# Moving the operands of the matmuls to other byte offsets in a Trainium2 layer kernel

## The chip, the cores and the metric

One core of one Trainium2 chip runs the whole kernel. The metric is the device time of one execution in microseconds, the median of several runs; less is better. TensorE does the matmuls (each is a weight load of the stationary operand and a pass of the moving one), VectorE and ScalarE work on tiles in SBUF, and SyncE issues the DMAs.

## The reference

One layer of an encoder in float32, for one sequence of 512 tokens and a width of 2048:

```python
mod = silu(c) @ w_ada + b_ada                       # six rows of 2048: sh1, sc1, g1, sh2, sc2, g2
h = rms_norm(x, norm1_g) * (1.0 + sc1) + sh1
proj = h @ w_in                                     # 2048 x 7168
o = concatenate([hgrn2(proj[:, :4096]), stick_breaking(proj[:, 4096:])])   # 8 heads each
x = x + g1 * (o @ w_out)                            # 2048 x 2048
h = rms_norm(x, norm2_g) * (1.0 + sc2) + sh2
gate, up = split(h @ w_ffn_in)                      # 2048 x 2*5632
x = x + g2 * ((silu(gate) * up) @ w_ffn_out)        # 5632 x 2048
```

## The kernel before

Every large product is computed from split operands: a float32 tile is copied by ScalarE into a rounded `hi` part and VectorE subtracts to get the `lo` part (`split`, lines 212 to 222, for weights; `split_o` and `split_to` for activations). Each product is then three matmuls of type float32r: hi by hi, hi by lo, lo by hi (`three`, line 227; `product`, line 908; `multiply`, line 1183). Every matmul has its own weight load.

The stages, in order of time: the values of the recurrent heads (banks `st`), the projections of the eight attention heads (`sb_project`, tiles `sbp`) with the attention work of the head before put between the matmuls, the projections of the eight recurrent heads (`hg_project`, `hg_gate`, tiles `hgf`, `hgq`, `hgg`) with the recurrent work between them, the output projection (`wo_part`), the first two column tiles of the feed-forward input (`first_part`, weights `wff`), the other 42 (`for f in range(2, FM)`, with a seven-product scheme after Strassen: products 1 to 7 of 24 matmuls with 256 columns), and the feed-forward output (`multiply`, again seven products, 12 units of 3 or 4 blocks). The order is written out by hand, with a clock of estimated times (`Clock`, `Timed`) that decides where the attention steps go.

Which operand is stationary differs. In `st` and `sbp` the activations `hhi`/`hlo` are stationary and the weights move (512 and 384 columns); in `hgf`, `hgq`, `hgg`, `wo` the weights are stationary and the activations (`hhi`/`hlo`, then `ohi`/`olo`) move, 512 columns; in the feed-forward input the weights are stationary and the operand blocks `opA` to `opD` move, 256 columns; in the feed-forward output the forms `opsA` to `opsC` are stationary and the weights move, 512 columns.

All these tiles lie in pools with fixed places in a partition. Pools on the left are stacked upwards: `const`, the weights' pool `wp` (four `raw` slots of 8192 bytes, three `hi` and three `lo` slots of 4096), then `hp` (slots `hhi` and `hlo`, 32,768 bytes each, used in turn by the split activations, the split output rows, `opB`/`opC` and `opsC`/`opsB`), then `fh` (slot `b1`: `opA`, later `opsA`) and `fg` (slot `b22`: `opD`). Pools on the right end at byte 229,344 and are stacked downwards. Each tile's size is rounded up to 32 bytes. The `hi` slots start at 43,808, 47,904 and 52,000, the `lo` slots at 56,096, 60,192 and 64,288, `hhi` at 68,384, `hlo` at 101,152, `b1` at 133,920, `b22` at 166,688: all 32 past a multiple of 256. Every block inside a tile is a multiple of 512 bytes long, so this holds for the start of every operand in them.

In the loop over `f` every fourth split of weights goes to a spare pair, `hi2` and `lo2` (`spare_here`, lines 1105 and 1106), in the right-hand pool `tp` at 215,008 and 219,104: 224 past a multiple of 256. The names in the trace show which: `ff_1h` and `ff_1l` are the ordinary tiles of product 1, `ff_1hi` and `ff_1lo` the spare pair. In the output stage the spare pair is a part of `opsB` that is not needed yet (`more`, line 1163, and `spare_there`, line 1165).

Of the kernel before, what the change touches and what calls it, by code (L numbers as in the profile page):

```python
# [10 lines left out]
F32 = mybir.dt.float32  # L11
F32R = mybir.dt.float32r
# [5 lines left out]
P = 128  # L18
D = 2048
KT = 16  # L20
T = 512
# [3 lines left out]
HT = 256  # L25
HALF = 8
CHUNKS = (3, 3, 4, 4, 4, 4)
ORDER = (2, 1, 7, 6, 4, 5, 3)
AHEAD = 300
SC2_EARLY = 8  # L30
HG_TASKS = 8
EARLY = 3
# [3 lines left out]
EPS = 1e-6  # L36
# [93 lines left out]
def trunk(ctx, tc, a):  # L130
    nc = tc.nc
    V, S, G = nc.vector, nc.scalar, nc.gpsimd
# [2 lines left out]

    const = ctx.enter_context(tc.tile_pool(name="const", bufs=1))
    wp = ctx.enter_context(tc.tile_pool(name="wp", bufs=3))
    xctx = ctx.enter_context(ExitStack())
    xop = xctx.enter_context(tc.tile_pool(name="xop", bufs=1, side="right"))
    hp = ctx.enter_context(tc.tile_pool(name="hp", bufs=1))  # L140
    dram = ctx.enter_context(tc.tile_pool(name="dram", bufs=1, space=bass.MemoryType.DRAM))
    psum = ctx.enter_context(tc.tile_pool(name="psum", bufs=4, space=bass.MemoryType.PSUM))

    def acc(name):
        return psum.tile([P, T], F32, tag="acc", name=name)
# [9 lines left out]
    ones = const.tile([P, P], F32, name="ones")  # L155
    G.memset(ones, 1.0)
    one = ones[:, 0:1]
    epsb = const.tile([P, 1], F32, name="epsb")
    G.memset(epsb, EPS)
    lead = const.tile([P, 2], F32, name="lead")  # L160
    left = [KT] * 6
    mod = const.tile([P, 96], F32, name="mod")
    gain1 = const.tile([P, KT], F32, name="gain1")
# [48 lines left out]
    def split(r, shape, name):  # L212
# [3 lines left out]
        else:  # L216
            hi = wp.tile(shape, F32R, tag="hi", name=name + "h")
            lo = wp.tile(shape, F32R, tag="lo", name=name + "l")
        with tc.high_priority(offset=AHEAD):
            S.copy(hi, r)  # L220
# [32 lines left out]
        newton(y, av, tmp)  # L253


    hhi = hp.tile([P, KT, T], F32R, tag="hhi", name="hhi")
    hlo = hp.tile([P, KT, T], F32R, tag="hlo", name="hlo")
    xo = xop.tile([P, KT, T], F32, tag="xo", name="xo")
    vctx = ctx.enter_context(ExitStack())
    vp = vctx.enter_context(tc.tile_pool(name="vp", bufs=1))  # L260
# [294 lines left out]
    def repairs():  # L555
# [8 lines left out]
        for i in range(2):  # L564
            items += [partial(fix, j) for j in range(6 + 4 * i, 10 + 4 * i)]
            items += [partial(settle, 6 + 4 * i, 10 + 4 * i, 6 + i, vh[:, :, i * T:i * T + T])]
        items += [load_masks] + [partial(ada, G1, k) for k in range(KT)] + [partial(ada, SC2, k) for k in range(SC2_EARLY)]
        yield from tasks_every(Y["task"], items)
# [211 lines left out]
    clock.start(hg_heads())  # L780
    rest = [partial(ada, SC2, k) for k in range(SC2_EARLY, KT)] + [partial(ada, SH2, k) for k in range(KT)]
    clock.start(tasks_every(Y["hgtask"], rest[:HG_TASKS]))
# [9 lines left out]
        gates[h] = SG  # L792


    ohi = hp.tile([P, KT, T], F32R, tag="hhi", name="ohi")
    olo = hp.tile([P, KT, T], F32R, tag="hlo", name="olo")
    last = NH - 1

    def split_o(k):
# [36 lines left out]
    fh = ctx.enter_context(tc.tile_pool(name="fh", bufs=1, reuse_waits="tile"))  # L836
    fg = ctx.enter_context(tc.tile_pool(name="fg", bufs=1, reuse_waits="tile"))
# [35 lines left out]

    early = fh.tile([P, 2, HALF, 2, HT], F32R, tag="b1", name="opA")
    H = {1: early[:, 0], 2: early[:, 1], 3: fg.tile([P, HALF, 2, HT], F32R, tag="b22", name="opD")}
    parts = {}

    def block(kh, th, j):  # L880
# [2 lines left out]
    def split_to(p, j, src):  # L883
        S.copy(H[p][:, j, 0], src)
        V.tensor_sub(H[p][:, j, 1], src, H[p][:, j, 0].bitcast(F32))

# [5 lines left out]
    def make_first(j):  # L892
        for kh in range(2):
            normed(kh, 0, j)
            split_to(1 + kh, j, block(kh, 0, j))
            parts[kh, 0, j] = H[1 + kh][:, j, 0], H[1 + kh][:, j, 1]

    def make_second(j):
# [6 lines left out]
        split_to(3, j, block(1, 1, j))  # L905
        parts[1, 1, j] = H[3][:, j, 0], H[3][:, j, 1]

    def product(out, w, p, first=False):
        whi, wlo = w
        for j in range(HALF):  # L910
            PE.matmul(out, whi[:, j], H[p][:, j, 0], start=first and j == 0, stop=False, skip_group_check=True)
            PE.matmul(out, whi[:, j], H[p][:, j, 1], start=False, stop=False, skip_group_check=True)
# [10 lines left out]
    for i, hs in enumerate(halves):  # L923
        out = acc(f"wo{m}h{i}")[:, 0:HT]
        n = 0
# [49 lines left out]
    for c in range(HALF + 1):  # L975
# [4 lines left out]
        if c == HALF - 1:  # L980
            with tc.high_priority(offset=AHEAD):
                hold(0)

    late = hp.tile([P, 2, HALF, 2, HT], F32R, tag="hhi", name="opB")
    later = hp.tile([P, 2, HALF, 2, HT], F32R, tag="hlo", name="opC")
    H.update({6: late[:, 0], 7: late[:, 1], 5: later[:, 0], 4: later[:, 1]})
    for j in range(HALF):
        V.tensor_sub(block(0, 0, j), block(0, 1, j), block(0, 0, j))
# [26 lines left out]
    def tap(src, name):  # L1015
        t = tp.tile([P, HT], F32, tag="tap", name=name, bufs=4)
        with tc.high_priority(offset=2 * AHEAD):
            S.copy(t, src)  # L1018
# [3 lines left out]
    places, blocks = [], [{} for _ in units]  # L1022
# [19 lines left out]
    yraw = []  # L1042

    def begin_second():
        places.append(fh.tile([P, 4, 4, 2, HT], F32R, tag="b1", name="opsA"))
        load_op(0, 0)
        load_y(0, 2)
        load_op(0, 1)
        load_y(0, 0)
        yraw.append(hp.tile([P, 3, 4, T], F32, tag="hhi", name="yraw0"))  # L1050
        load_y(0, 1)
        load_y(0, 3)
        load_op(0, 2)
        load_op(0, 3)
        places.append(hp.tile([P, 4, 4, 2, HT], F32R, tag="hlo", name="opsB"))
        for q in range(4, 7):
            load_op(0, q)
        yraw.append(fg.tile([P, 2, 4, T], F32, tag="b22", name="yraw"))

    rest += [partial(ada, G2, k) for k in range(KT)]  # L1060

# [37 lines left out]
    later = []  # L1099
# [9 lines left out]
    count[0] = 0  # L1109
    with tc.high_priority(offset=AHEAD):  # L1110
        hold(1)
# [3 lines left out]
    for f in range(2, FM):  # L1115
# [4 lines left out]
        w1, w2 = operand(A11, f"ff{f}_1"), operand(A12, f"ff{f}_2")  # L1120
        with tc.high_priority(offset=AHEAD):
            V.tensor_add(S1, A21, A22)
# [22 lines left out]
        up = tp.tile([P, T], F32, tag="up", name=f"up{f}", bufs=1)  # L1145
        with tc.high_priority(offset=2 * AHEAD if f == FM - 1 else 0):
            V.tensor_add(sg[:, 0:HT], B, ta)
# [82 lines left out]
    for u, (c, i) in enumerate(units):  # L1230
        def dst(th, j, dh):
            return O[:, 2 * th + j, dh * 1024 + i * T:dh * 1024 + i * T + T]

        def ready(th, dh):
            if c == last_c:
                outs.extend((8 * dh + 4 * i + m, th) for m in range(4))

        first, final = c == 0, c == last_c
        if final and i == 0:
            for g in range(4):  # L1240
                nc.sync.dma_start(place(7 * c + 7 + g).bitcast(F32).rearrange("p n h t -> p n (h t)"), x1d[:, 4 * g:4 * g + 4])
        y = blocks[u]
        t2 = (T2 if u else yraw[0][:, 2])[:, 0:CHUNKS[c]]
        load_y(u + 1, 2)
        load_y(u + 1, 0)
        for q, p in enumerate(ORDER):
            out = {2: B[i], 7: C, 4: C}.get(p, A)
            raw = {2: y[2], 1: y[0], 7: y[1], 6: t2, 4: y[2], 5: y[0], 3: y[3]}[p]
            sums = {7: [(y[1], y[3], y[1])], 6: [(t2, y[3], y[0])], 4: [(y[2], y[2], t2)]}.get(p, ())
            if p == 7:  # L1250
                with tc.high_priority(offset=AHEAD):
                    for k0 in range(0, CHUNKS[c], 2):
                        ks = slice(k0, min(k0 + 2, CHUNKS[c]))
                        V.tensor_sub(y[0][:, ks], y[1][:, ks], y[0][:, ks])
            multiply(out, c, q, raw, p in (1, 7) or p == 2 and first, u, sums)
            if final:
                some_out(3)
            for j in range(2):
                if p == 1:
                    onto(dst(0, j, 0), A[j], first)  # L1260
                    if final:
                        V.tensor_add(dst(0, j, 0), B[i][j], dst(0, j, 0))
                elif p == 7:
                    onto(dst(1, j, 1), C[j], first)
                elif p == 6:
                    onto(dst(1, j, 0), A[j], first)
                elif p == 4:
                    V.tensor_add(dst(1, j, 0), C[j], dst(1, j, 0))
                elif p == 5:
                    onto(dst(1, j, 1), A[j], False)  # L1270
                elif p == 3:
                    if first:
                        S.copy(dst(0, j, 1), A[j])
                    else:
                        V.tensor_add(dst(0, j, 1), A[j], dst(0, j, 1))
            if p == 1:
                ready(0, 0)
                if final:
                    slots += [t[:, h * HT:h * HT + HT] for t in B[i] for h in range(2)]
            elif p in (4, 5, 3):  # L1280
                ready(*{4: (1, 0), 5: (1, 1), 3: (0, 1)}[p])
            if p == 7:
                load_y(u + 1, 1)
            if p == 3:
                load_y(u + 1, 3)
            if u == 0 and q == 6:
                places.append(hp.tile([P, 4, 4, 2, HT], F32R, tag="hhi", name="opsC"))
            if q < 4 and i == (c == 0):
                load_op(c + 1, q)
            if i == 1 and 1 <= q < 4:  # L1290
                load_op(c + 1, q + 3)
# [60 lines left out]
```

## Time and profile before

| | |
|---|---|
| median of 3 runs | 2299.24 us (2299.24 to 2306.46) |
| profiled execution | 2301.37 us |
| its span, first to last instruction | 2299.2 us |
| TensorE busy | 2249.4 us, 98% of the span, 14,171 matmuls |
| VectorE busy | 1917.8 us, 83% |
| ScalarE busy | 1160.6 us, 50% |
| mean granted TensorE clock | 0.994 of 2.4 GHz |
| DMA | 437.69 MB, mean 190 GB/s |

Matmuls are pipelined: the profile gives one a duration of some 280 to 400 ns, while the next one starts 110 to 230 ns after it. So the rate is read from the starts, and a busy TensorE says only that it did not stand still for long.

### The profile page before, as it was taken

To read this page: it belongs to the slowest core of one execution; us is meant where nothing else is said; L and a number is where in the kernel's file an instruction comes from. 1 tells how busy PE (TensorE), PEld (TensorE's weight loads), DVE (VectorE), ACT (ScalarE), POOL (GpSimd) and SP (SyncE) were. 2 spreads that over 40 slices of the span, in tenths; PEclk is the share of its full clock that TensorE was granted. 3 is DMA by queue.
4 is the path that set the end of the run, shared out by engine and by line. 5 is a ranking of instruction groups with operands and counts; after the bars stand their busy time and mean duration, and the time that the engine had idled before them with its cause. 6 is when DMAs were issued, how large, how long until landed. Compare 5 with 4: busy or idle time off the path is not lost.

```text
span 2299.2 us, 35729 instructions
## 1 busy us (share of the span) xinstructions
PE 2249.4 (98%) x14171; PEld 2050.2 (89%) x14171; DVE 1917.8 (83%) x2566; ACT 1160.6 (50%) x2015; POOL 10.7 (0%) x25
## 2 busy tenths in 40 slices
PE   7999899999999999999999999999999999999999
PEld 6899899888888788999999999999999977778787
DVE  8887779999888865699899988888888778888888
ACT  4316666565655522564454445454545544544453
POOL 0000000000000000000000000000000000000000
PEclk9999999999999999999999999999999999999999
DMA  9885546853322386346555645454443486665452
GB/s 368 319 317 218 174 145 227 304 183 111 128 93 74 130 303 214 105 151 225 189 204 185 220 143 175 143 174 143 150 160 129 166 314 232 238 220 213 154 200 76
DMA packets 114978, 437.69 MB, mean 190 GB/s; under 512 B 9822, under 2 KB 58236, under 8 KB 76796
## 3 DMA queue, kind: packets, MB, share of 16 engines
q1 hardware_dynamic: 114812, 435.42, 53.0%
q8 instruction: 111, 1.82, 0.3%
q14 instruction: 55, 0.45, 0.1%
HBM read 386.61 MB, written 48.77 MB: 189 GB/s over the span
## 4 chain that ended last, share of the span: by engine, by line
PE 77%; DVE 13%; DMA 3%; issue 3%; ACT 3%; SPq 0%; DVEq 0%; ACTq 0%
PE ffA L93 18%; PE foA L93 9%; PE ffC L93 9%; PE sbp L93 7%; PE wo L93 7%; PE foC L93 4%; PE ffB L93 4%; PE st L93 4%; PE hgf L93 4%; PE hgq L93 3%; PE hgg L93 3%; DMA opd<-fhi 1%; DVE ada L180 1%; DVE yraw L1190 1%; PE l L93 1%
## 5 line engine op out<-in xcount | busy, mean ns | idle before, releaser
L180 DVE SCALAR_TENSOR_TENSOR ada<-ada,cond 128x2048 f32<-128x2048 f32 x95 | 216.8, 2286 | 54.5 <-DMA ada<-in_w_ada 54.3
L93 PE MATMUL ffA<-opD,ff_3h 128*128 128x256 f32 x512 | 93.9, 284 | 1.8 <-ACT u L1018 1.7
L93 PE MATMUL ffA<-opB,ff_6h 128*128 128x256 f32 x512 | 94.1, 284 | 1.0 <-ACT ff_6h L220 1.0
L93 PE MATMUL ffB<-opA,ff_2h 128*128 128x256 f32 x512 | 93.5, 283 | 0.0
L93 PE MATMUL ffC<-opC,ff_4h 128*128 128x256 f32 x512 | 93.5, 283 | 0.0
L93 PE MATMUL ffA<-opC,ff_5h 128*128 128x256 f32 x496 | 90.7, 283 | 0.8 <-ACT b L1018 0.8
L93 PE MATMUL ffA<-opA,ff_1h 128*128 128x256 f32 x496 | 90.6, 283 | 0.0
L93 PE MATMUL ffC<-opB,ff_7h 128*128 128x256 f32 x496 | 90.6, 283 | 0.0
L221 DVE TENSOR_TENSOR wfo_0l<-wfo,wfo_0h 128x1024 fp32r<-128x1024 f32 x48 | 58.7, 1224 | 37.9 <-ACT wfo_0h L220 37.5
L93 PEld LDWEIGHTS ffA<-opD,ff_3h 128*128 128x128 f32 x512 | 79.7, 192 | 2.4 <-ACT u L1018 2.4
L93 PEld LDWEIGHTS ffA<-opB,ff_6h 128*128 128x128 f32 x512 | 80.1, 193 | 1.3 <-ACT ff_6h L220 1.2
L93 PEld LDWEIGHTS ffC<-opC,ff_4h 128*128 128x128 f32 x512 | 79.7, 192 | 0.0
L93 PEld LDWEIGHTS ffB<-opA,ff_2h 128*128 128x128 f32 x512 | 79.7, 192 | 0.0
L220 ACT CAST wfo_0h<-wfo 128x1024 fp32r<-128x1024 f32 x48 | 50.6, 1054 | 57.5 <-PE foA L93 50.4
L1092 ACT CAST fhi<-forms 128x512 fp32r<-128x512 f32 (+1 forms) x63 | 43.6, 692 | 68.5 <-DMA opd<-fhi 59.2
L93 PEld LDWEIGHTS ffA<-opC,ff_5h 128*128 128x128 f32 x496 | 77.2, 192 | 1.0 <-ACT b L1018 1.0
L93 PEld LDWEIGHTS ffC<-opB,ff_7h 128*128 128x128 f32 x496 | 77.3, 192 | 0.0
L93 PEld LDWEIGHTS ffA<-opA,ff_1h 128*128 128x128 f32 x496 | 77.2, 192 | 0.0
L93 PE MATMUL ffA<-opB,ff_6l 128*128 128x256 f32 x256 | 72.7, 284 | 0.0
L93 PE MATMUL ffC<-opC,ff_4l 128*128 128x256 f32 x256 | 72.4, 283 | 0.0
L93 PE MATMUL ffA<-opD,ff_3l 128*128 128x256 f32 x256 | 72.4, 283 | 0.0
L93 PE MATMUL ffB<-opA,ff_2l 128*128 128x256 f32 x256 | 72.4, 283 | 0.0
(1646 smaller groups left out, 7764.6 us busy)
## 6 DMA issues: line engine op xcount, KB each, us to landing
ada<-in_w_ada SPq DMA_DIRECT2D x95, 1024.0 KB, 5.2
wfo<-in_w_fo SPq DMA_DIRECT2D x16, 1024.0 KB, 5.9
yraw<-in_w_fo SPq DMA_DIRECT2D x16, 1024.0 KB, 4.8
fix<-in_w_fix SPq DMA_DIRECT2D x14, 1024.0 KB, 5.6
opd<-forms SPq DMA_DIRECT2D x44, 256.0 KB, 4.3
opd<-fhi SPq DMA_DIRECT2D x42, 256.0 KB, 4.3
opsC<-opd SPq DMA_DIRECT2D x10, 1024.0 KB, 5.1
opsA<-opd SPq DMA_DIRECT2D x9, 1024.0 KB, 7.2
```

Source lines behind the costliest of these rows:

```text
L93: self.engine.matmul(out, lhsT, rhs, **kw)
L180: V.scalar_tensor_tensor(w, w, 1.0, row, op0=ALU.mult, op1=ALU.mult, accum_out=col)
L220: S.copy(hi, r)
L221: V.tensor_sub(lo, r, hi.bitcast(F32))
L1092: S.copy(hi, R[:, q])
L1190: V.tensor_sub(*(t[:, k0:k0 + w] for t in (d, e, g)))
```

## The change

The `const` pool loses `epsb` (now a column of a 24-column tile in a new pool at the right edge) and `lead` grows from 2 to 34 columns. A helper `offset` allocates a tile 64 elements (256 bytes) longer than needed and returns a view that starts `shift` elements into it. The split activations, the split output rows, the feed-forward operands and the forms of the output stage are allocated with it. Loops, instructions and their operands' shapes stay as they are.

```diff
+ROOM = 64
+OFF_H, OFF_O, OFF_F, OFF_X = 8, 32, 16, 48
...
+    edge = ctx.enter_context(tc.tile_pool(name="edge", bufs=1, side="right"))
...
+    def offset(pool, shape, dtype, tag, name, shift):
+
+        n = int(np.prod(shape[1:]))
+        t = pool.tile([P, n + ROOM], dtype, tag=tag, name=name)[:, shift:shift + n]
+        axes = "abcd"[:len(shape) - 1]
+        sizes = dict(zip(axes, shape[1:]))
+        return t.rearrange(f"p ({' '.join(axes)}) -> p {' '.join(axes)}", **sizes)
...
-    epsb = const.tile([P, 1], F32, name="epsb")
-    G.memset(epsb, EPS)
-    lead = const.tile([P, 2], F32, name="lead")
+    epsw = edge.tile([P, 24], F32, name="epsw")
+    G.memset(epsw, EPS)
+    epsb = epsw[:, 0:1]
+    lead = const.tile([P, 34], F32, name="lead")
...
-    hhi = hp.tile([P, KT, T], F32R, tag="hhi", name="hhi")
-    hlo = hp.tile([P, KT, T], F32R, tag="hlo", name="hlo")
+    hhi = offset(hp, [P, KT, T], F32R, "hhi", "hhi", OFF_H)
+    hlo = offset(hp, [P, KT, T], F32R, "hlo", "hlo", OFF_H)
...
-    ohi = hp.tile([P, KT, T], F32R, tag="hhi", name="ohi")
-    olo = hp.tile([P, KT, T], F32R, tag="hlo", name="olo")
+    ohi = offset(hp, [P, KT, T], F32R, "hhi", "ohi", OFF_O)
+    olo = offset(hp, [P, KT, T], F32R, "hlo", "olo", OFF_O)
...
-    early = fh.tile([P, 2, HALF, 2, HT], F32R, tag="b1", name="opA")
-    H = {1: early[:, 0], 2: early[:, 1], 3: fg.tile([P, HALF, 2, HT], F32R, tag="b22", name="opD")}
+    early = offset(fh, [P, 2, HALF, 2, HT], F32R, "b1", "opA", OFF_F)
+    H = {1: early[:, 0], 2: early[:, 1], 3: offset(fg, [P, HALF, 2, HT], F32R, "b22", "opD", OFF_F)}
...
-    late = hp.tile([P, 2, HALF, 2, HT], F32R, tag="hhi", name="opB")
-    later = hp.tile([P, 2, HALF, 2, HT], F32R, tag="hlo", name="opC")
+    late = offset(hp, [P, 2, HALF, 2, HT], F32R, "hhi", "opB", OFF_F)
+    later = offset(hp, [P, 2, HALF, 2, HT], F32R, "hlo", "opC", OFF_F)
...
-        places.append(fh.tile([P, 4, 4, 2, HT], F32R, tag="b1", name="opsA"))
+        places.append(offset(fh, [P, 4, 4, 2, HT], F32R, "b1", "opsA", OFF_X))
...
-        yraw.append(hp.tile([P, 3, 4, T], F32, tag="hhi", name="yraw0"))
+        yraw.append(offset(hp, [P, 3, 4, T], F32, "hhi", "yraw0", 0))
...
-        places.append(hp.tile([P, 4, 4, 2, HT], F32R, tag="hlo", name="opsB"))
+        places.append(offset(hp, [P, 4, 4, 2, HT], F32R, "hlo", "opsB", OFF_X))
...
-        yraw.append(fg.tile([P, 2, 4, T], F32, tag="b22", name="yraw"))
+        yraw.append(offset(fg, [P, 2, 4, T], F32, "b22", "yraw", 0))
...
-                places.append(hp.tile([P, 4, 4, 2, HT], F32R, tag="hhi", name="opsC"))
+                places.append(offset(hp, [P, 4, 4, 2, HT], F32R, "hhi", "opsC", OFF_X))
```

An element is 4 bytes, so the four offsets are 32, 128, 64 and 192 bytes.

## Rows read from the trace of the kernel before

**Rows 1.** The page: TensorE's busy time, and the chain of work that ended last.
```profile
PE 2249.4 (98%) x14171; PEld 2050.2 (89%) x14171; DVE 1917.8 (83%) x2566; ACT 1160.6 (50%) x2015; POOL 10.7 (0%) x25
...
PE 77%; DVE 13%; DMA 3%; issue 3%; ACT 3%; SPq 0%; DVEq 0%; ACTq 0%
```

**Rows 2.** Busy time by stretch (from:to in us, length, engines, clock, DMA).
```profile
12.00:101.00 89.00, 89.00 (x386) 73.32 (x387) 80.58 (x115) 38.43 (x53) 0.00 (x0) 1.00 0.96 359
101.00:439.00 338.00, 327.16 (x1893) 313.15 (x1891) 274.80 (x373) 178.14 (x431) 0.00 (x0) 0.97 0.62 225
439.00:768.00 329.00, 327.53 (x1675) 275.31 (x1675) 287.25 (x541) 199.53 (x441) 9.05 (x16) 1.00 0.37 132
768.00:956.00 188.00, 183.97 (x871) 152.42 (x869) 117.46 (x147) 60.67 (x97) 0.00 (x0) 1.00 0.59 209
956.00:1004.00 48.00, 47.61 (x390) 46.83 (x388) 48.00 (x129) 45.76 (x110) 0.00 (x0) 1.00 0.30 102
1004.00:1849.00 845.00, 838.33 (x7052) 836.89 (x7052) 726.56 (x822) 419.79 (x612) 0.00 (x0) 1.00 0.50 175
1849.00:2295.00 446.00, 435.45 (x1917) 352.05 (x1916) 378.55 (x432) 211.91 (x269) 0.00 (x0) 1.00 0.56 202
```

**Rows 3.** TensorE's waits: for whom, total us, times, longest.
```profile
PE st L93 <- ACT hhi L309: 11.8, 1, 11.8
PE foA L93 <- ACT O L1205: 3.6, 1, 3.6
```

**Rows 4.** Timeline of TensorE: first matmuls of products 5, 4, 1, 2.
```profile
1502.87 0.40 PE L93 MATMUL ffA<-opC,ff_5h 128*128 128x256 f32 x2
...
1505.75 0.40 PE L93 MATMUL ffC<-opC,ff_4h 128*128 128x256 f32 x2
...
1511.51 0.39 PE L93 MATMUL ffA<-opA,ff_1hi 128*128 128x256 f32 x2
...
1514.23 0.40 PE L93 MATMUL ffB<-opA,ff_2h 128*128 128x256 f32 x2
```

**Rows 5.** Groups with ordinary and spare tiles (busy us, mean ns of one).
```profile
L93 PE MATMUL ffA<-opA,ff_1h 128*128 128x256 f32 x496 | 90.6, 283 | 0.0
...
L93 PE MATMUL ffA<-opA,ff_1hi 128*128 128x256 f32 x176 | 30.5, 276 | 0.0
...
L221 DVE TENSOR_TENSOR ff_5l<-ffS,ff_5h 128x1024 fp32r<-128x1024 f32 x31 | 37.8, 1218 | 0.0
...
L221 DVE TENSOR_TENSOR ff_5lo<-ffS,ff_5hi 128x1024 fp32r<-128x1024 f32 x11 | 13.4, 1219 | 0.5 <-ACT ff_5hi L220 0.5
```

**Rows 6.** Timeline: six starts of 384 columns, nine and seven of 512.
```profile
300.07 0.33 PE L93 MATMUL sbp<-wsb_6l,hhi 128*128 128x384 f32 x1
...
301.11 0.33 PE L93 MATMUL sbp<-wsb_6l,hhi 128*128 128x384 f32 x1
...
900.04 0.39 PE L93 MATMUL wo<-ohi,wo_8l 128*128 128x512 f32 x1
...
902.08 0.39 PE L93 MATMUL wo<-ohi,wo_8l 128*128 128x512 f32 x1
...
1999.62 1.75 PE L93 MATMUL foC<-opsB,opsC 128*128 128x512 f32 x7
2001.21 0.39 PE L93 MATMUL foA<-wfo_0h,opsC 128*128 128x512 f32 x1
```

**Rows 7.** VectorE in two parts of the input stage, and its `ada` products there.
```profile
1004.00:1340.00 336.00, 329.33 (x2750) 327.89 (x2750) 311.30 (x355) 164.15 (x241) 0.00 (x0) 0.99 0.55 198
1340.00:1849.00 509.00, 509.00 (x4304) 509.00 (x4303) 415.26 (x468) 255.64 (x372) 0.00 (x0) 1.00 0.46 160
...
L180 DVE SCALAR_TENSOR_TENSOR ada<-ada,cond 128x2048 f32<-128x2048 f32 x16 | 36.6, 2290 | 14.1 <-DMA ada<-in_w_ada 14.1
```

**Rows 8.** Timeline: four passes of two transposes in the output stage.
```profile
2242.00 0.60 PE L98 MATMUL foB<-ident,O 128*128 128x128 f32 x4
```

## The prediction

> **What bounds the kernel now.** I read the engine totals first, then the busy times by stage, then single starts of matmuls, because the first two leave only one place for a change of addresses to act. TensorE is busy 98% of the span, and the chain that ended last is 77% TensorE [rows 1]. By stage, at a granted clock of 0.97 to 1.00 of 2.4 GHz throughout [rows 2], it is the limit in the feed-forward input stage (1004 to 1849 us, 838 of 845 us busy), nearly so in the head projections (101 to 439 and 439 to 768), the output projection (768 to 956) and the feed-forward output stage (1849 to 2295). Two stages have another engine at its limit as well: 12 to 101 us runs at 359 GB/s with the DMA engines 96% busy, and in 956 to 1004 us VectorE is busy for all 48 us. Waits of TensorE for other engines are short, the longest in total but for the start being 3.6 us [rows 3]. So what counts is how densely the matmuls start.
>
> That is seen in the starts. In the feed-forward input stage a product is 24 matmuls of 256 columns. Product 5, whose weights are in the ordinary tiles (L217, L218), takes 1505.75 - 1502.87 = 2.88 us, which is 120 ns each; product 1, whose weights are in the spare pair `hi2`/`lo2` (L1106), takes 1514.23 - 1511.51 = 2.72 us, 113.3 ns each [rows 4]. Nothing else differs in kind. The two groups' mean durations say the same: 283 against 276 ns [rows 5]. At 2.4 GHz 256 columns are 106.7 ns, so the ordinary tiles cost 13.3 ns over streaming and the spare ones 6.7. The wider stages pay the 13.3 too: 384 columns (160.0) start every 173.3 ns, 512 columns (213.3) every 226.7 [rows 6].
>
> The difference is one of address. In this kernel the ordinary weight tiles and all moving operands of the stage start 32 bytes past a multiple of 256 in their partition; the spare pair starts 224 past one. Moving minus stationary is 0 in the slow case and, modulo 256, +64 in the fast one.
>
> **The change, part by part.** No instruction is added or taken away but for the length of one memset and two small tiles. Removing `epsb` (32 bytes) and lengthening `lead` (by 128) moves everything on the left by 96, and the 96-byte `edge` pool moves the right side down, so all weight tiles, spare ones too, come to start at 128 modulo 256. The operands then stand at fixed distances from them.
>
> *First feed-forward operands, +64.* All 7 products get the distance that the spare pair has now. The stage has 42 x 7 = 294 products, every fourth spare: 73, so 221 x 24 = 5304 matmuls go from 120.0 to 113.3 ns: 35.4 us. Is VectorE ready for that? In 1340 to 1849 us it is busy 415 of 509 [rows 7], and three quarters of 4304 matmuls by 6.67 ns are 21.6 us: all kept. In 1004 to 1340 us, with the 16 `ada` products of 2.29 us each, it is busy 311 of 336; the 13.8 us to be had there would leave it 11 us of slack, and it waits 14.1 us for `ada` rows alone [rows 7]. I keep half, 6.9. If that cover is gone altogether, 21.6 remain. Together 28.5 us. What is late next is the `lo` half of the weights (L221 on VectorE).
>
> [...]
>
> *Act forms, +192.* In the output stage the roles are exchanged: the forms (`ops`) are stationary and the weights move, so moving minus stationary is -192, again +64 modulo 256. 12 units x 7 x 24 or 18 matmuls make 1848; a quarter of them have their weights in the spare part of `opsB` itself (L1165), which moves along with the forms and stays at distance 0. 1386 x 6.67 ns = 9.2 us. VectorE is busy 378.6 of 446 us there [rows 2] and late at times, so I keep three quarters: 6.9.
>
> *Split output rows, +128, and split activations, 32.* No row has these distances. `ohi`/`olo` serve 720 matmuls of 512 and 96 of 256 columns; `hhi`/`hlo` move in 1152 of 512 columns (439 to 768 us, distance +32) and are stationary in 1536 of 384 columns (101 to 439 us, distance -32). From both sides: a matmul can lose its whole 13.3 ns, or pay it twice if the streams meet more often, as they might. I take the 6.67 of the nearest row, the spare pair: 5.4 us x 0.9 (VectorE is busy 117 of 188 us there [rows 2]) = 4.9 for the output projection; 7.7 x 3/4 = 5.8 and 10.2 x 3/4 = 7.7 for the two head stages, where attention steps between the projections wait on VectorE and ScalarE. The share of three quarters is my estimate from VectorE's 81 to 87% there.
>
> *The first 101 us and the 48 us before the feed-forward stage:* 384 matmuls each. DMA in the one and VectorE in the other have no room [rows 2], so 0; with that cover gone 2.6 us each.
>
> *VectorE and ScalarE at new addresses:* the subtraction to the spare `lo2` takes 1219 ns and to the ordinary tile 1218 [rows 5], so 0. No row shows a weight tile that starts on a multiple of 64; what that gives or takes is left to rivals B and E.
>
> Sum: 28.5 + 6.9 + 4.9 + 5.8 + 7.7 = 53.8 us. The profiled execution took 2301.4 us (span 2299.2 and 2.2 around it): 2247.6. It is 2.1 over the median of the runs, 2299.24, so the forecast for the median is 2245.
>
> **Rivals.**
>
> *B, the rest goes too.* The 6.7 ns left in the spare pair may come from operands that start 32 bytes off a multiple of 64, as all of them do now and nearly none will (only the split activations). For it: the two extras are 1 and 2 times 16 columns' time, that of 64 bytes. Against: transposes, whose two operands (`ident2` and `O`) are also 32 past a multiple of 64, start 109 ns apart ((0.60 - 0.27)/3 [rows 8]) for two passes of 53.3, 2 ns over streaming. With 2 ns left everywhere, ordinary matmuls save 11.3 and spare ones 4.6: second part of the input stage 36.5 + 4.9 = 41, first part held by VectorE at 12; 14 for the output stage, 8, 10 and 13 for the rest: 99 us, so 2301.4 - 99 - 2.1 = 2200.
>
> [...]
>
> *C, only the known distance pays.* If the period is 128 and not 256, +128 is 0 again, and 32 may be too near; with the output stage lost to VectorE, 28.5 us remain: 2301.4 - 28.5 - 2.1 = 2271.
>
> *D, the change doesn't act.* The spare pair could owe its 6.7 ns to its place at the far end of the partition (215,008 and up) rather than to its distance. Against: the slow case is the same for moving operands at 68,384, 101,152, 133,920 and 166,688. Then 2299. [...]
>
> *E, slower.* At 32, 128 or 192 bytes the two streams meet once more than at 0, and each matmul of the other four stages pays 13.3 ns more: (1536 + 1152 + 816 + 1386) x 13.3 = 65 us, all on TensorE's path, against 28.5 gained: 2301.4 + 65 - 28.5 - 2.1 = 2336. It decides from 28.5 / 4890 = 5.8 ns, that is 512-column matmuls starting over 232.5 ns apart. For it: the distances are unmeasured. Against: distance 0 should be the worst for two streams of one rate.
>
> **Numbers.** Forecast 0.43, B 0.27, C 0.15, D 0.07, E 0.08. Faster by over 0.3% (6.9 us, about what a measurement of this kernel can tell from no change): the forecast, B and C, 0.85; the same: D, 0.07; slower: E, 0.08. The likeliest case alone reaches from 2231 (all 67.9 us kept) to 2258 (half of what the four other stages bring, 12.7, lost). The range goes on above to C with the rest of the first part and a third of the second lost to VectorE (6.9 + 7.2: 2285), and below to B with 8 us more, since its shares are estimates: 2192.
>
> **What would show it.** Right: input-stage products of 2.72 us with ordinary and spare weights alike, output stage at 220 ns but for a quarter at 227, VectorE's share up by some 3 points in 1340 to 1849, and its `lo` subtractions among TensorE's waits before 1340. B shows as products under 2.65 us. Wrong: products still of 2.88 us (D), or 512-column starts over 227 ns (E). Equal counts of instructions on every engine are assumed; another order of the work would make this comparison void.

## The result and the profile after

The changed kernel takes 2312.3 us in the median (2311.74 to 2315.48), the kernel before 2303.57 in the same comparison: ratio 1.0044, 95% interval 1.0032 to 1.0056. It is slower by some 10 us, 67 us above the forecast of 2245. Its profiled execution has a span of 2309.7 us against 2299.2.

The chain that ended last in the changed kernel, by engine; then its busy times by stage (columns as in [rows 2], the bounds at this kernel's own ends of stages):

```profile
PE 79%; DVE 14%; issue 3%; DMA 3%; ACT 2%; SPq 0%; DVEq 0%; ACTq 0%
```
```profile
12.00:103.00 91.00, 91.00 (x386) 73.02 (x386) 80.33 (x115) 38.45 (x53) 0.00 (x0) 1.00 0.93 351
...
439.00:771.00 332.00, 331.08 (x1665) 274.02 (x1664) 286.63 (x539) 199.11 (x439) 9.04 (x16) 1.00 0.36 130
771.00:965.00 194.00, 190.06 (x872) 153.93 (x871) 118.23 (x147) 60.82 (x96) 0.00 (x0) 0.99 0.57 203
...
1013.00:1858.00 845.00, 835.47 (x7057) 833.09 (x7056) 726.23 (x824) 419.09 (x612) 0.00 (x0) 1.00 0.50 175
1858.00:2306.00 448.00, 438.73 (x1915) 351.92 (x1914) 378.85 (x433) 211.79 (x269) 0.00 (x0) 1.00 0.55 201
```

Beside [rows 2] the lengths read: first stage 91 for 89, recurrent heads' projections 332 for 329, output projection 194 for 188, feed-forward input 845 for 845, output stage 448 for 446. The stages in which 512 columns move each grew; the stage that was to give 28.5 us gave nothing. TensorE is as busy, and the chain as much its own (79% for 77%, [rows 1]).

The timeline of the changed kernel's TensorE (start, length, last the count of a group): starts of 384 columns in `sbp` and of 512 in `wo`; first matmuls of products 6, 7 (spare pair) and 5 of the input stage; a run in the output stage.

```profile
300.08 0.34 PE L95 MATMUL sbp<-wsb_6l,hhi 128*128 128x384 f32 x1
...
301.12 0.34 PE L95 MATMUL sbp<-wsb_6l,hhi 128*128 128x384 f32 x1
...
908.55 0.40 PE L95 MATMUL wo<-ohi,wo_8l 128*128 128x512 f32 x1
...
910.65 0.39 PE L95 MATMUL wo<-ohi,wo_8l 128*128 128x512 f32 x1
...
1507.68 0.40 PE L95 MATMUL ffA<-opB,ff_6h 128*128 128x256 f32 x2
...
1510.51 0.40 PE L95 MATMUL ffC<-opB,ff_7hi 128*128 128x256 f32 x2
...
1513.34 0.40 PE L95 MATMUL ffA<-opC,ff_5h 128*128 128x256 f32 x2
...
2008.10 2.93 PE L95 MATMUL foC<-opsB,opsC 128*128 128x512 f32 x12
2010.87 0.40 PE L95 MATMUL foA<-wfo_0h,opsC 128*128 128x512 f32 x1
```

Products on ordinary and spare weights are alike now, as forecast, but at 2.83 us, 117.8 ns a start: between the 2.88 and the 2.72 of [rows 4]. Three ordinary products won 2.2 ns a start and the spare one lost 4.5, so the sum is near nothing. Starts of 512 columns, 226.7 ns before [rows 6], are 233.3 apart in `wo` (nine in 2.10 us; `hgq` has the same) and 230.8 in the output stage (2.77/12, although this run, both operands moved alike, stands at distance 0 as before; in grid2 below, twelve at distance 0 right after a run at 160 take 2.74 to 2.77 us as well). Those of 384 kept 173.3.

### The profile page after: what moved, and what is told of

Read it like the earlier page. It is cut to its first block, busy times and chain, and to the rows that moved or that the text cites. A ratio compares the mean times of both kernels' runs of the same rounds, so it can differ in the third digit from the quotient of the medians.

```text
span 2309.7 us, 35730 instructions
## 1 busy us (share of the span) xinstructions
PE 2259.8 (98%) x14171; PEld 2045.0 (89%) x14171; DVE 1918.2 (83%) x2566; ACT 1159.9 (50%) x2015; POOL 10.7 (0%) x25
## 4 chain that ended last, share of the span: by engine, by line
PE 79%; DVE 14%; issue 3%; DMA 3%; ACT 2%; SPq 0%; DVEq 0%; ACTq 0%
PE ffA L95 18%; PE ffC L95 9%; PE foA L95 9%; PE sbp L95 8%; PE wo L95 7%; PE ffB L95 4%; PE foC L95 4%; PE st L95 4%; PE hgf L95 4%; PE hgq L95 3%; PE hgg L95 3%; DMA opd<-fhi 1%; DVE yraw L1202 1%; PE l L95 1%; DVE ada L192 1%
## 5 line engine op out<-in xcount | busy, mean ns | idle before, releaser
L1104 ACT CAST fhi<-forms 128x512 fp32r<-128x512 f32 (+1 forms) x63 | 43.6, 692 | 82.7 <-DMA opd<-fhi 64.3
L1105 DVE TENSOR_TENSOR forms<-forms,fhi 128x512 fp32r<-128x512 f32 (+1 forms) x63 | 48.9, 777 | 28.2 <-ACT fhi L1104 28.2
```

What stands on the lines that cost most here:

```text
L1104: S.copy(hi, R[:, q])
L1105: V.tensor_sub(R[:, q].bitcast(F32R), R[:, q], hi.bitcast(F32))
```

## The experiments

Each kernel of the whole layer is compared with the kernel before on the same chip; of the grids, which leave the layer out, only the starts are read. "Distance" is stationary minus moving start, in bytes modulo 256: 192 is what the prediction called +64. The theories are numbered in the expectations.

**grid.** A kernel of its own: runs of 24 matmuls at each distance, the layer left out.

```
for n in (512, 256):
    for m in (0, 32):
        for d in range(0, 1024, 32):
            stream(n, m, d, 24)        # stationary at m + d, moving at m
```

> This kernel leaves the whole layer out and measures the disputed cost by itself: streams of 24 equal matmuls (512 and 256 columns, float32r, each with its own weight load), no other engine at work, the moving operand at 0 or 32 bytes modulo 1024 and the stationary one at 32 distances of 0 to 992 bytes from it. Theory 1, the cost depends on the distance and on where the operands start in a stretch of 64 bytes: starts at equal distance differ between moving operands at 0 and at 32, and for 32 the distances 0 and -64 (stationary behind by 64) give 120.0 and 113.3 ns at 256 columns, 0 gives 226.7 at 512. Theory 2, only the distance counts, over 1024 bytes and not 256: both moving operands give one curve, with distances 128 and 896 near 237 ns and 384 and 640 near 229 at 512 columns. Theory 3, the slower starts come from VectorE, ScalarE or DMA, whose tiles moved too: with them silent all distances start at one interval, within 1 ns.

Timeline of TensorE; a row is one run, and the interval is the next row's start less its own, over 24. `ai` is distance 0, `aj` 32, `ak` 64, `ao` 192, `ap` 224:

```profile
66.46 5.61 PE L43 MATMUL nzma_ai<-mov,sta 128*128 128x512 f32 x24
71.91 5.75 PE L43 MATMUL nzma_aj<-mov,sta 128*128 128x512 f32 x24
77.50 5.76 PE L43 MATMUL nzma_ak<-mov,sta 128*128 128x512 f32 x24
...
99.92 5.67 PE L43 MATMUL nzma_ao<-mov,sta 128*128 128x512 f32 x24
105.42 5.76 PE L43 MATMUL nzma_ap<-mov,sta 128*128 128x512 f32 x24
...
401.12 3.03 PE L43 MATMUL nyma_ai<-mov,sta 128*128 128x256 f32 x24
403.99 3.00 PE L43 MATMUL nyma_aj<-mov,sta 128*128 128x256 f32 x24
...
418.19 2.99 PE L43 MATMUL nyma_ao<-mov,sta 128*128 128x256 f32 x24
421.02 3.00 PE L43 MATMUL nyma_ap<-mov,sta 128*128 128x256 f32 x24
```

For 512 columns distance 0 is the best (settled 226.7 ns), 192 costs 2 more (5.50/24 = 229), the others 6.7 to 7.5 more (5.59/24 = 233). For 256 columns 0 is, with 160, the worst: 120.0, against 117.1 to 118.3 at the others, 192 among them (117.8). With the moving operand on a multiple of 64 or 32 past one the curve is the same, and it repeats every 256 bytes: one curve, as theory 2 has it, with another period; theories 1 and 3 fall. So address acts, by distance, with no other engine at work; but no run here shows the spare pair's 113.3.

**realign** and **offsets** take the change apart: the moved `const` pool without the offsets, and the offsets with the old `const` pool.

```diff
-ROOM = 64
-OFF_H, OFF_O, OFF_F, OFF_X = 8, 32, 16, 48
+ROOM = 0
+OFF_H, OFF_O, OFF_F, OFF_X = 0, 0, 0, 0
```

> The changed kernel with all four offsets and the extra room at 0: tiles, spare pair too, start at 128 modulo 256 and all distances are 0. Theory 1: ordinary matmuls of the input stage no longer start every 120.0 ns, nor those of 512 columns every 226.7; which way is open (some 117 to 126 ns, some 229 to 238). Theory 2: 120.0 and 226.7 as before, and the spare pair at 120.0 too, so 1752 x 6.7 ns = 12 us more than before, 2315. Theory 3: irregular starts that differ from one product to the next.

```diff
...
-    epsw = edge.tile([P, 24], F32, name="epsw")
...
-    lead = const.tile([P, 34], F32, name="lead")
+    epsb = const.tile([P, 1], F32, name="epsb")
...
+    lead = const.tile([P, 2], F32, name="lead")
```

> The changed kernel with the const pool and the right edge as before: weights start at 32 modulo 256, the offsets 32, 128, 64 and 192 stay. Theory 1: ordinary weights of the input stage have the start and the distance that the spare pair had, so 113.3 ns: 35 us less there, less than 2280 in all. Theory 2: the same distances as in the changed kernel, so its 118 ns and 229 to 238 ns again, about 2312. Theory 3: 120 and 226.7 back, since VectorE's and ScalarE's tiles are back, about 2303.

realign takes 2309.58 us, ratio 1.0033 (1.0018 to 1.0047): 7 us over the kernel before, where theory 2 has 12. Every operand, the spare pair's too, is at distance 0, and the spare pair, still at the far end of the partition, lost its 113.3 ns. Input stage of realign, by busy time and in the timeline (first matmuls of product 3, on the spare pair, and of the ordinary 1 and 2, 2.88 us each):

```profile
1002.00:1861.00 859.00, 851.58 (x7061) 849.96 (x7060) 728.68 (x824) 420.02 (x613) 0.00 (x0) 1.00 0.49 172
```
```profile
1495.17 0.40 PE L95 MATMUL ffA<-opD,ff_3hi 128*128 128x256 f32 x2
...
1498.05 0.40 PE L95 MATMUL ffA<-opA,ff_1h 128*128 128x256 f32 x2
...
1500.93 0.40 PE L95 MATMUL ffB<-opA,ff_2h 128*128 128x256 f32 x2
```

The stage lasts 859 us for 845, of which 1752 spare matmuls by 6.7 ns explain 11.7. offsets takes 2312.11 us, ratio 1.0045 (1.003 to 1.006), as the whole change: the offsets do it, and ordinary weights at 128 or at 32 modulo 256 are alike (2.83 us a product in both). The spare pair stands at distance 128 there, and its products take 2.85.

**all_fast** is the kernel before with the feed-forward operands alone moved, and the spare pair kept at distance 192 from them.

```diff
+ROOM = 64
+OFF_H, OFF_O, OFF_F, OFF_X = 0, 0, 16, 0
...
+    edge.tile([P, 48], F32, name="pad")
```

> The kernel before with the first feed-forward operands alone at +64, and the right side moved by 192 so that the spare pair has the same distance; all else stays at distance 0. No product of the input stage is then at distance 0. Theory 4: the stream has nothing to settle it and starts every 117.8 ns, as in the changed kernel: 5304 x 2.2 gained and 1752 x 4.5 lost, 4 us less than before, about 2299; or, if what the stage before leaves behind holds, 113.3 from the start until the first wait. Rival (distance alone): 117.8 throughout, the same 2299. The 226.7 of the other stages stays, so the rest of the changed kernel's loss (some 13 us) is gone.

It takes 2299.42 us, ratio 0.9996 (0.9986 to 1.0006). Busy times of its output projection and input stage, and starts of its products 7 (spare) and 5:

```profile
768.00:954.00 186.00, 183.36 (x867) 152.09 (x866) 115.41 (x147) 58.80 (x94) 0.00 (x0) 1.00 0.60 212
...
1001.00:1846.00 845.00, 836.87 (x7060) 834.56 (x7059) 726.90 (x825) 418.37 (x614) 0.00 (x0) 1.00 0.50 175
```
```profile
1498.25 0.40 PE L95 MATMUL ffC<-opB,ff_7hi 128*128 128x256 f32 x2
...
1501.08 0.40 PE L95 MATMUL ffA<-opC,ff_5h 128*128 128x256 f32 x2
```

With the other operands back at distance 0 the loss is gone: the output projection lasts 186 us for the change's 194. So the whole slow-down lies in the stages of 512 columns. And the input stage stays at 845 with nearly every product at 2.83: moving all seven products together destroys the short interval.

**grid2** and **grid3** ask where 113.3 ns comes from: runs at one distance after runs at another, in steps of 16 and of 8 bytes, with the layer left out.

```
stream(256, 0, 160, 24, "r"); stream(256, 0, 0, count, "p"); stream(256, 0, 192, 60, "t")
```

> Leaves the whole layer out, as the first grid. There the distance stationary minus moving of 192 modulo 256 gave 117.8 ns at 256 columns, while the spare pair of the kernel before, at the same distance, starts every 113.3. Here each stream of 60 at a distance (0 to 240 by 16) follows 12 matmuls at distance 0; others follow streams at 32 to 224, or 1, 2 or 4 matmuls at 0; one stream of 400 follows 12 at 0; two have the stationary tile at the far end of the partition. Theory 4, the interval depends on what ran before (the weight load and the moving stream keep the phase that they start with): after distance 0 the distance 192 starts every 113.3 ns, after others every 117.8, and the 400 tell how long it holds. Theory 5, the far place makes it: 113.3 only with the far tile, after either. If neither, 117.8 throughout, and something else of the kernel before makes the 113.3, such as the pattern of three (hi hi, hi lo, lo hi) or the work of other engines.

Timeline of grid2, runs at distance 192 after 160 and one and two matmuls at 0, and one of 400 after twelve:

```profile
564.77 0.28 PE L46 MATMUL py_aa<-mov,sta 128*128 128x256 f32 x1
564.88 7.23 PE L46 MATMUL ty_am<-mov,sta 128*128 128x256 f32 x60
...
574.83 0.40 PE L46 MATMUL py_aa<-mov,sta 128*128 128x256 f32 x2
575.07 6.97 PE L46 MATMUL ty_am<-mov,sta 128*128 128x256 f32 x60
...
596.35 45.51 PE L46 MATMUL uy_am<-mov,sta 128*128 128x256 f32 x400
```

The same distance has two intervals: 117.8 ns (7.23 us for 60, 0.28 of them the last one's) and 113.3 (6.97), and the second holds for 400 matmuls in a row. Which one a run takes depends on what ran just before (theory 4). Distance 0 is not the only way in: a run at 64 took 113.3 too, and the run at 192 behind it. Theory 5 falls: on a weight tile at the far end of the partition the interval was 113.3 after 0 and after 160, but the near tile reaches it as well.

> Leaves the whole layer out. Streams at distances 0 to 252 (512 columns by 8, 384 by 16, 256 by 8 bytes), each after a stream at distance 0 that has had 24 or 36 matmuls to settle. Theory 4 (history): at 256 columns 192 starts every 113.3 ns, the others stay at 116.7 to 120 or show second intervals too; at 384 columns distance 0 and 32 both give 173.3; at 512 no distance is below 226.7 unless it too has a second interval. Rival (the distance alone sets the interval): the numbers of the first two grids again, 117.8 for 192.

grid3 finds no distance at which 512 columns start closer than 226.7 ns (0, 16, 40, 120, 144, 216 and 240 reach it), nor 384 closer than 173.3. For 256 columns only 168 and 192 reach 113.3 after distance 0; 24 is the worst with some 122.

**relock** puts one operand, that of product 3, back to distance 0 in all_fast, so that every seventh product runs at 0 and the next ones follow it.

```diff
-..."b22", "opD", OFF_F)}
+..."b22", "opD", 0)}
```

> As all_fast, but the operand of product 3 (the last of each seven) stays at distance 0, so that each iteration has 24 matmuls at distance 0 and 144 at 192. Theory 4: product 3 at 120.0, the other six at 113.3: 6048 x 113.3 + 1008 x 120 = 806 us against 835 before, 29 us less, about 2275, less what VectorE holds back in the first 330 us. Rival (distance alone): six at 117.8: 833 us, about 2302.

It takes 2299.98 us, ratio 0.9995 (0.9984 to 1.0006). Product 2 is still 2.83 us long, and so are the others that follow at 192:

```profile
1497.42 0.40 PE L95 MATMUL ffB<-opA,ff_2h 128*128 128x256 f32 x2
...
1500.25 0.40 PE L95 MATMUL ffA<-opB,ff_6h 128*128 128x256 f32 x2
```

A miss: a run at 0 isn't enough. In the kernel before the step from 0 to 192 changed the weight's address, here the moving operand's.

**grid4** and **kick** test that. grid4 steps from 0 to 192 in both ways, again with the layer left out; kick is all_fast with the spare pair at distance 0.

```diff
-    edge.tile([P, 48], F32, name="pad")
+    edge.tile([P, 32], F32, name="pad")
```

> Only matmuls of 256 columns on constant data, the layer left out; runs at distance 192 from stationary to moving operand that begin right after a run at distance 0. Theory 6: the interval of 113.3 ns is entered when the stationary operand moves from distance 0 to 192, not when the moving operand does. It expects 113.3 in the runs where only the weight changed (cs, ck, es, fs) and 117.8 in those where the moving operand changed (cm, cr, em, fm), at every length of the run at 0 of two or more. Theory 7: what decides is the phase that the run at 0 itself has, given by what came before it, and not which operand changes. It expects the same of cs and cm and of es and em, and a result that turns with the length of the run at 0 or with what ran before it (after a run at 32 as after a run at 192).

> As all_fast (feed-forward operands at distance 192 from the ordinary weights), but with the spare pair of weight tiles put at the operands' own address modulo 256, so every fourth product runs at distance 0, and the step back to 192 changes the weight and not the operand. Theory 6: products on ordinary tiles start every 113.3 ns, those on the spare pair every 120.0; against the kernel before that is 5,304 x 6.67 less and 1,752 x 6.67 more, 23.7 us less, some 2280. Theory 7: with the stream in the phase that it had in all_fast the ordinary ones stay at 117.8, the spare ones go to 120.0, and the sum is 5,304 x 2.2 less and 1,752 x 6.67 more, nothing: the time of the kernel before within 4 us.

Timeline of grid4: `csz` and `cmz` are 24 matmuls at 0; in `csq` the weight is the one moved to 192, in `cmq` the operand; `b_ga` is 48 at 192 by the weight, after 24 at 160:

```profile
48.17 3.04 PE L49 MATMUL csz_ah<-mov,sta 128*128 128x256 f32 x24
51.05 8.32 PE L49 MATMUL csq_ai<-mov,sta 128*128 128x256 f32 x72
...
78.57 3.04 PE L49 MATMUL cmz_an<-mov,sta 128*128 128x256 f32 x24
81.45 8.64 PE L49 MATMUL cmq_ao<-mov,sta 128*128 128x256 f32 x72
...
480.67 5.61 PE L49 MATMUL b_ga<-mov,sta 128*128 128x256 f32 x48
```

From start to start 8.32 us for 72 is 113.3 ns, 8.64 is 117.8. Moving the operand, alone or with the weight, never gave the short interval, after 2 to 96 matmuls at 0. Moving the weight alone gave it after 8 or more, but not after 2, 3, 4 or 6, and not after 24 that followed a stretch at 32 and had not settled (117 to 125 ns a start instead of 120). The runs at 192 after 24 at 160, whose starts swing between some 115 and 125 ns to the end, took it in 10 cases of 29, `b_ga` (113.3 ns) among them. So theory 6 has the condition right and its lengths wrong: in every case the weight moved, and (the part of theory 7 that holds) the state that the run before leaves behind decides. A settled run at 0 led into it all 16 times; it is a sure way in, not the only one.

kick takes 2299.2 us, ratio 0.9978 (0.9963 to 0.9993): theory 6's starts with theory 7's time. Its chain of waits over one stretch of the input stage (start, length, what):

```profile
1579.67 2.99 DMA opd<-fhi
...
1582.74 0.04 ACT fhi L1104
...
1583.27 1.05 ACT ff_1hi L232
1584.31 0.27 ACT c L1030
...
1584.63 3.09 PE ffC L95 x24
1587.72 5.70 PE ffA L95 x48
1593.42 2.72 PE ffB L95 x24
...
1601.52 6.91 DMA wu33r<-in_w_fi
...
1618.97 3.01 DMA opd<-fhi
```

Ordinary products do take 2.72 us here, 154 of 221 of them, but the chain is no longer TensorE's alone: over the span its share falls from 77% [rows 1] to 65%. The cast of the next part of the forms (L1104) waits until the transfer of the last part has read its one buffer; behind it on ScalarE stands the copy that frees TensorE's accumulator (`c`, L1030); TensorE waits (12 times for `c` in the stage, 4.2 us), its weights' slot comes free later, and the load for the unit after next with it (`wu33r`, 1601.52). This comes round every two units (a unit is one turn of the loop over `f`, seven products), 39.3 us apart (1579.67, 1618.97). TensorE's own work for two units, fourteen products, 3.5 of them spare, was 10.5 x 2.88 + 3.5 x 2.72 = 39.8 us in the kernel before [rows 4], just longer than that loop; in kick it is 10.5 x 2.72 + 3.5 x 2.88 = 38.6, shorter. That this loop sets the pace is a reading of the chain, which kick2 below tests. After each wait the products run at 117.8 or worse (3.09; 5.70 for two, the second on the spare pair) until the spare pair has settled the stream again. ScalarE's wait for that transfer in kick from 1203 us on, and the input stage, 846 us long:

```profile
ACT fhi L1104 <- DMA opd<-fhi: 73.1, 30, 3.7
```
```profile
1003.00:1849.00 846.00, 828.84 (x7055) 822.88 (x7054) 724.32 (x824) 415.93 (x614) 0.00 (x0) 0.99 0.50 175
```

**kick2** and **before_fhi** give that cast a second buffer, in kick and in the kernel before.

```diff
-                hi = tp.tile([P, b - a, HT], F32R, tag="fhi", name=f"fhi{f}_{a}", bufs=1)
+                hi = tp.tile([P, b - a, HT], F32R, tag="fhi", name=f"fhi{f}_{a}", bufs=2)
```

> As kick, with a second buffer for the high halves of the act forms, so that ScalarE's cast for the next part no longer waits until the transfer of the last part has read the buffer (73 us of such waits in kick between 1203 and 1850 us, with the copies that free TensorE's accumulators queued behind). Theory 8: in kick the starts did save their 18 us, and a loop through weight load, VectorE, this cast and the copy behind it, as long as two units of the stage, took them back as waits of TensorE; a shorter loop gives most of it back, 12 to 24 us under the kernel before, 2279 to 2290. Theory 9: the limit is VectorE's own work or the weight loads, which the second buffer leaves as they are: as kick, 2297 to 2302.

> The kernel before with the same second buffer and nothing else. Theory 8: with starts every 120 ns TensorE is the limit of the stage (840 of 847 us busy), so at most its remaining waits there of some 7 us can go, 2295 to 2303. Theory 9: nothing, 2302. If this kernel gains as much as kick2 does against kick, the buffer does it alone and the starts count for nothing.

kick2 takes 2282.46 us, ratio 0.9905 (0.9884 to 0.9926), faster than both kernels; before_fhi 2301.55, ratio 0.9994 (0.9985 to 1.0003). So neither half gives it alone, as theory 8 has it. kick2's input stage, ScalarE's wait there from 1200 us on, and the chain of waits in the stretch shown of kick, which is TensorE throughout, with an ordinary and a spare product:

```profile
1000.00:1829.00 829.00, 820.06 (x7059) 818.21 (x7058) 726.33 (x825) 420.99 (x615) 0.00 (x0) 1.00 0.49 178
```
```profile
ACT fhi L1104 <- DMA opd<-fhi: 14.6, 16, 2.9
```
```profile
1581.31 2.72 PE ffB L95 x24
...
1589.47 2.88 PE ffA L95 x24
```

The scheduler that builds the program puts VectorE's instructions in another order with the second buffer, the same one in kick2 and before_fhi. So the gain over kick is that of buffer and order together, and at the old intervals both together gave nothing.

## Why the prediction was wrong

**The failed step** is "All 7 products get the distance that the spare pair has now ... 5304 matmuls go from 120.0 to 113.3". They got the distance, and went to 117.8. The 113.3 was no property of a distance alone: three products at 0 settled the stream, and the weight's move to 192 put it on the short interval, as all 16 moves of the weight alone from a settled run did in grid4. Taking the products off 0 took away what the spare pair lived on: its products went from 2.72 to 2.83 us, in all_fast too. "Nothing else differs in kind" overlooked it: in [rows 4] the spare product stands behind ordinary ones. In the changed kernel that is 5304 x 2.2 ns won and 1752 x 4.5 lost, 3.8 us on paper, which the stage's length doesn't show.

**The second failure, enough by itself for the sign:** "I take the 6.67 of the nearest row" for the unmeasured distances of the 512-column stages. Distance 0, taken as their worst, is their best; the distances of the changed kernel cost them 2 to 7 ns more. That is what rival E supposed, at half its price of 13.3: `hgq` and `wo` passed its deciding 232.5 ns, and from first to last start the two stages lost 4.5 and 5.6 us where 5.8 and 4.9 were to be won; the output stage lost 1.8, where 6.9 were to be won. What misled was one rule for all lengths: 256, 384 and 512 columns each pay 13.3 ns at distance 0 by the forecast's count, but only for 256 is that near the worst. The count is an estimate: at distance 0 the starts, 120.0, 173.3 and 226.7 ns apart, grow by 53.3 ns for each 128 columns [rows 4, rows 6], which leaves 13.3 over 106.7, 160.0 and 213.3; no run shows a matmul that only streams. For 384, at distance 32 in the changed kernel, nothing could come of the forecast 7.7 us: they start every 173.3 ns at 32 as at 0, and no distance of grid3 is better.

**The first 101 us** were set at 0 because DMA had no room, with 2.6 if that cover went. They cost some 2: from first to last start they take 90.9 and 91.5 us in the changed kernel and offsets, 88.3 to 89.9 in the seven kernels with distance 0 there. DMA's share fell from 0.96 to 0.93 and TensorE was busy all the while (91 of 91 us), so DMA's lack of room hid little of the loss.

**Keeping the gain.** "Is VectorE ready for that?" was the wrong question. At 415 of 509 us busy [rows 7] it was ready; kick's starts were worth 23.7 us and the stage returned none, because of a wait for one buffer on ScalarE. [rows 3] could not show it: by kick's 39.3 us the loop was half a microsecond shorter than TensorE's own time, so TensorE hardly waited. ScalarE's waits did show it. In the kernel before, the wait for this transfer is its longest in total in the input stage (1004 to 1849 us):

```profile
ACT fhi L1092 <- DMA opd<-fhi: 59.2, 37, 4.7
```

To go by kick, then, even the right intervals would not have brought these 28.5 us.

**The rivals.** B fell with the grid: alignment to 64 changes nothing. Its 2 ns rest on counting 109 ns as two passes of 53.3, which is a reading of the author's that no run shows: the four entries of [rows 8] are four transposes of one matmul each (the stage has 64 of both), not four passes of two. The shortest interval of any run here at 256 columns is 113.3 ns, where B needed 108.7. C's period of 128 isn't there. D's premise, that the far place sets the spare pair apart, fell with realign, where the far pair took 120.0 ns. E named the sign, and of its four stages three lost; it got 0.08. Its 65 us of loss were 11.9, and the 28.5 that it set against them never came. That two streams meet is shown by no run.

The trace of before could have warned of three things: the rule for one length was carried to others without a row, no spare product ran without ordinary ones before it, and ScalarE waited for the transfer (59.2 us).

**Open:** what inside TensorE or its reads makes distance and history count. The runs give the function, not the cause. The input stage of kick2 gives 16 us of the 23.7 (829 for 845), with 189 of 221 ordinary products at 2.72 us; why not with all was not taken further.

## What to carry over

An interval read from one instruction stream belongs to that stream with its neighbours (the spare pair's 113.3 ns became 117.8 once its neighbours stood at its distance): before giving all others the same address, measure a stream made only of it, at each length of the moving operand. Bound an unmeasured distance from both sides of zero and let the sign stay open. And when the limiting engine is to get faster, look for the loops that are only just hidden by it: a single buffer behind a queue that also frees accumulators is one (here 39.3 us a turn against TensorE's 39.8).

## Unexpected in the hardware

- The interval of a weight load and a matmul in float32r depends on the two operands' distance modulo 256 bytes: 113.3 to some 122 ns for 256 columns, 173.3 to some 177 for 384, 226.7 to some 234 for 512; for 256 and 512 it is the same whether the moving operand starts at a multiple of 64 or 32 past one.
- At distance 192 and 256 columns there are two steady intervals, 113.3 and 117.8 ns; what ran just before decides, and the shorter one lasted for 400 matmuls.
- A settled run at distance 0 led into the shorter one every time that the weight's address alone changed (16 of 16 in grid4), and never when the moving operand's did. After a run at 160 it came in 10 of 29 cases.
